# A decoder layer's second norm with its mean removed through the weights: w_down's rows centred while they are split

## The chip, the cores and the metric

The kernel runs on one core of one Trainium2 chip. The metric is the device time of one execution in microseconds (us); three runs of the kernel before gave 368.61, 368.86 and 369.11 us, and the median, 368.86 us, is the time to compare with. The engines are named as in the profile: PE is TensorE's matmul, PEld its weight load, DVE is VectorE, ACT is ScalarE, POOL is GpSimd, SP is the engine whose queue issues most transfers.

## The reference, cut to what matters

One layer over 256 positions of width 1024, all in float32. The change concerns the last two lines, the feed-forward part (FFN) and its norm:

```python
x = layer_norm(alpha * x + mix, ln1_g, ln1_b)          # first norm: its result is x1 below
u = causal_dwconv3(x @ w_up)                           # w_up 1024 x 5632
f = (silu(u[..., :2816]) * u[..., 2816:]) @ w_down     # w_down 2816 x 1024
x = layer_norm(alpha * x + f, ln2_g, ln2_b)            # second norm

def layer_norm(x, g, b):
    mu = mean(x); var = mean((x - mu) ** 2)            # over the 1024 columns
    return (x - mu) * rsqrt(var + 1e-5) * g + b
```

If each row of `w_down` has its own mean over the 1024 columns taken out, every row of `f @ w_down` has mean zero; if `alpha * x` has its mean taken out too, the sum in the second norm has mean zero, and its variance is the mean of its squares.

## The kernel before, in words

**Weights.** Float32 products are made of three matmuls in a faster type: every matrix is split in a high half `h` (a rounding copy on ACT, `split_h`) and a low half `l` (the rest, `raw - h`, on DVE, `split_l`). The weights come in 1 MB chunks of two units each, a unit being 128 x 1024 numbers: two groups of 128 columns of w_up, or two groups of 128 rows of w_down. A chunk is loaded by one transfer of SP's queue into a buffer `raw` (`issue_dma`); there are three such buffers (`RAW_BUFS = 3`), and nine for the halves (`HL_BUFS = 9`). A buffer is given to a later chunk when the instructions that read it have ended, and the loads start in the order of the list that `plan` makes.

**FFN.** The 22 groups of 128 channels are `i = 0..21`. For each, TensorE runs a gate piece (`g`, unit of chunk `ug`), a value piece (`v`, chunk `uv`) and, three groups later, a `down` (`d`, chunk `dn`) that multiplies the finished group with its 128 rows of w_down into four PSUM banks. `seq` is this list, two groups to a pair `c = 1..10`: g, v, d, g, v, d. `plan` lists the chunks of a pair as ug(c), uv(c), dn(c-1). `slot(k)` writes the work that stands beside piece k: on ACT some stages of the FFN (`fb` is the sum of the two halves of a product out of PSUM, `fc` the convolution's first tap, `fs` the silu, `f` the high half of the result), then `split_h` for the piece five ahead (six from piece 20 on), on DVE `split_l` for the piece before that, then DVE's stages. Every engine works through its own list in order. The last eight `down` (`TAIL = 8`, units of dn 7 to 10) come after all gate and value pieces.

**Second norm.** `finish(t)` handles the rows 0..127 (t = 0) and 128..255 (t = 1). For each piece of columns, DVE adds `ALPHA * x1` to the products and takes statistics (`bn_stats`); `norm_stats` joins them (`bn_aggr`) and POOL makes the power -1/2 of the variance; then come two passes of DVE, `(r - mean) * g` and `r * rstd + b`, and the transfers to `out`. For t = 1 the products of the columns 512..1023 are made last, 256 at a time (tile `e`), so that only the last 256 columns' addition and statistics, the joining and the passes follow the last matmul.

Of the kernel before, what the change touches and what calls it, by code (L numbers as in the profile page):

```python
# [8 lines left out]
F32 = mybir.dt.float32  # L9
# [6 lines left out]
P = 128  # L16
# [36 lines left out]
OFF_B, OFF_C, OFF_H, OFF_G = 3 * AW, 3 * AW + CW, 3 * AW + 2 * CW, 3 * AW + 3 * CW  # L53
TAIL = 8


def plan():

# [79 lines left out]
def layer_kernel(ctx: ExitStack, tc: tile.TileContext, x, wpack, cpack, ln1_g, ln1_b, ln2_g, ln2_b, out):  # L138
# [27 lines left out]
    raws = []  # L166
    XR_CHUNK = 20

    def issue_dma(c):
        while len(raws) <= c and len(raws) < len(chunks):  # L170
            i = len(raws)
            t = wp.tile([P, CHUNK], F32, tag="raw", name=f"raw{i}", bufs=RAW_BUFS)
            raws.append(t)
            for a, b, off in blocks[i]:
                nc.sync.dma_start(t[:, a:b], wpack[off:off + P * (b - a)].rearrange("(p n) -> p n", p=P))
            if i == XR_CHUNK:
                nc.sync.dma_start(xr, x[0].rearrange("(t p) d -> p t d", p=P))
# [5 lines left out]
    def split_start(u):  # L183
        issue_dma(units[u]["chunk"] + RAW_BUFS - 1)
        alloc(u, "h", "wh")
        alloc(u, "l", "wl")

    def split_h(u):

        issue_dma(units[u]["chunk"] + RAW_BUFS - 1)  # L190
        alloc(u, "h", "wh")
        nc.scalar.activation(units[u]["h"], raw_of(u), AF.Copy)  # L192

    def split_l(u):

        alloc(u, "l", "wl")
        nc.vector.tensor_tensor(units[u]["l"], raw_of(u), units[u]["h"].bitcast(F32), op=ALU.subtract)  # L197

    def raw_of(u):
        un = units[u]  # L200
# [524 lines left out]
        nc.vector.scalar_tensor_tensor(o, r, mv[:, 0:1], g, op0=ALU.subtract, op1=ALU.mult)  # L725
        nc.vector.scalar_tensor_tensor(o, o, mv[:, 3:4], b, op0=ALU.mult, op1=ALU.add)

    def norm_second(r, mv, ln, cs):
        nc.vector.scalar_tensor_tensor(r[:, cs], r[:, cs], mv[:, 3:4], ln[:, 1, cs], op0=ALU.mult, op1=ALU.add)

    def norm_first(r, mv, ln, cs):
        nc.vector.scalar_tensor_tensor(r[:, cs], r[:, cs], mv[:, 0:1], ln[:, 0, cs], op0=ALU.subtract, op1=ALU.mult)
# [175 lines left out]
    def take(n):  # L908
# [4 lines left out]
                pending.remove((stage, i))  # L913
        return out


    seq = []
    for c in range(1, NP // 2):
# [6 lines left out]
                seq.append(("d", d, U[("dn", d // 2)] + d % 2))  # L925
    for d in range(NP - TAIL, NP):
        seq.append(("t", d, U[("dn", d // 2)] + d % 2))
    done = {"h": cur["u"] - seq[0][2], "l": cur["u"] - seq[0][2]}
    def slot(k, stages):


        for st, i in stages:
            FFN[st][0](i)
        la = LA if k < 20 else LA + 1
        while done["h"] < min(len(seq), k + la + 2):
            split_h(seq[done["h"]][2])
            done["h"] += 1
        while done["l"] < min(len(seq), k + la + 1):
            split_l(seq[done["l"]][2])
            done["l"] += 1  # L940
        for st, i in stages:
            FFN[st][1](i)

    tail_from = next(k for k, s in enumerate(seq) if s[0] == "t")
    for k, (kind, i, u) in enumerate(seq[:tail_from]):
# [15 lines left out]
        if kind == "v":  # L961
            stages.insert(0, (0, i))
            pending.extend([(st, i) for st in (1, 2, 3)])
        slot(k, stages)


    def finish(t):
        r = x1[:, t]
        stats = tmp.tile([P, 4, 6], F32, tag="stats", name=f"rstats{t}", bufs=2)
        if t == 0:  # L970
            for k in range(TAIL):
                down(NP - TAIL + k, (t,))
                slot(tail_from + k, take(2))
            assert not pending
            for nh in range(2):
                residual(t, nh, dacc[t][nh], x1, r, stats, nh, nh * 512, nh * 512 + 512)
        else:
            for i in range(NP - TAIL, NP):
                down(i, (t,), (0,))
            nc.vector.scalar_tensor_tensor(r[:, 512:1024], x1[:, t, 512:1024], ALPHA, dacc[t][1], op0=ALU.mult, op1=ALU.add)  # L980
            for c in range(2):
                residual(t, 0, dacc[t][0], x1, r, stats, c, c * 256, c * 256 + 256)
            for c in range(2, 4):
                bank = ps_pair(f"e{c}")[:, 0]
                for i in range(NP - TAIL, NP):
                    down_part(i, bank, c)
                nc.vector.tensor_tensor(r[:, c * 256:c * 256 + 256], r[:, c * 256:c * 256 + 256], bank[:, 0:256], op=ALU.add)
                nc.vector.bn_stats(stats[:, c, :], r[:, c * 256:c * 256 + 256])
        mv = norm_stats(r, stats, 2 if t == 0 else 4)
        if t == 0:  # L990
            for c in range(2):
                cc = slice(c * 512, (c + 1) * 512)
                norm_apply(r[:, cc], r[:, cc], mv, ln2[:, 0, cc], ln2[:, 1, cc])
                nc.sync.dma_start(out[0, t * P:(t + 1) * P, cc], r[:, cc])
            return
        for c in range(2):
            norm_first(r, mv, ln2, slice(c * 512, c * 512 + 512))
        for cc, queue in ((slice(0, 640), nc.sync), (slice(640, D), nc.scalar)):
            norm_second(r, mv, ln2, cc)
            queue.dma_start(out[0, t * P:(t + 1) * P, cc], r[:, cc])  # L1000

    for t in range(2):
        finish(t)
# [42 lines left out]
```

## Time and profile before

| what | value |
|---|---|
| median of three runs | 368.86 us (368.61 to 369.11) |
| the profiled execution's own time | 369.0 us |
| its span, first to last instruction | 367.1 us |
| TensorE busy | 358.0 us, 98% of the span |
| VectorE busy | 294.9 us, 80% |
| ScalarE busy | 217.0 us, 59% |
| weight loads, 1 MB each | 55, median 4.9 us from issue to landing |

A line of the groups reads: line of the kernel, engine, operation, tile written <- tiles read, shapes, count, then busy time and mean of one in ns, then the idle time before these instructions and who ended it. A line of the timeline reads: start, duration, engine, line, operation, tiles, count, and in brackets the idle time before it with who ended it. A line of the table by stretches gives the stretch, its length, then each engine's busy time with its count of instructions (PE, PEld, DVE, ACT, POOL), the granted TensorE clock as a share of full speed, the transfers' share and GB/s. A line of the waits gives who waited for whom, the total, how often, and the longest.

### The profile page before, as it was taken

How to read it: one execution, taken by the hardware profiler on the slowest of the kernel's cores; microseconds unless marked ns; L12 is line 12 of the kernel's file. 1: busy time of each engine (PE TensorE's matmuls, PEld its weight loads, DVE VectorE, ACT ScalarE, POOL GpSimd, SP SyncE). 2: the span in 40 equal slices, each digit the busy share in tenths (PEclk: the TensorE clock that was granted, in tenths of full speed). 3: DMA queues.
4: the chain of work that ended last, by engine and by line, in shares of the span. 5: the costliest groups of instructions: out<-in, count | busy, mean ns of one | idle time of the engine just before them, and what ended most of it. 6: DMA issues, size and time to landing. Idle time of an engine off the chain costs nothing.

```text
span 367.1 us, 5335 instructions
## 1 busy us (share of the span) xinstructions
PE 358.0 (98%) x2022; PEld 312.2 (85%) x2022; DVE 294.9 (80%) x510; ACT 217.0 (59%) x372; POOL 7.0 (2%) x26
## 2 busy tenths in 40 slices
PE   8999999999999999999999999999999999999991
PEld 7888888888888899988888888888888888888891
DVE  4696887788895679869769988987869696999784
ACT  4685776747867654634266666575657566676300
POOL 2000000000000000102000000000000000000000
PEclk9999999999999999999999999999999999999998
DMA  7978565333853634596360835448182645662011
GB/s 263 356 292 318 180 225 211 114 114 129 331 214 130 221 124 137 190 357 224 124 223 12 341 121 221 153 193 309 46 334 90 254 140 204 228 237 108 0 59 57
DMA packets 11241, 69.63 MB, mean 190 GB/s; under 512 B 1232, under 2 KB 1616, under 8 KB 4176
## 3 DMA queue, kind: packets, MB, share of 16 engines
q1 hardware_dynamic: 10496, 67.00, 50.0%
q0 software_dynamic: 576, 2.10, 1.8%
q8 instruction: 16, 0.26, 0.3%
q10 hardware_dynamic: 144, 0.20, 0.1%
q14 instruction: 9, 0.07, 0.1%
HBM read 68.24 MB, written 1.05 MB: 189 GB/s over the span
## 4 chain that ended last, share of the span: by engine, by line
PE 97%; DVE 1%; DMA 1%; DVEq 0%; SPq 0%; issue 0%
PE pb L333 20%; PE pb L340 10%; PE g L333 8%; PE d L305 5%; PE d L306 5%; PE d L307 5%; PE g L340 4%; PE q L555 3%; PE k L555 3%; PE v L555 3%; PE b L333 2%; PE y L326 2%; PE y L325 2%; PE y L324 2%; PE c L333 2%; PE o L307 2%
## 5 line engine op out<-in xcount | busy, mean ns | idle before, releaser
L197 DVE TENSOR_TENSOR wl<-raw,wh 128x1024 fp32r<-128x1024 f32 x90 | 109.8, 1221 | 23.3 <-ACT wh L192 22.7
L192 ACT ACTIVATE wh<-raw 128x1024 fp32r<-128x1024 f32 x90 | 94.5, 1055 | 22.7 <-DMA raw<-in_wpack 22.6
L333 PE MATMUL pb<-x1T,wh 128*128 128x512 f32 x320 | 76.2, 390 | 0.0
L333 PEld LDWEIGHTS pb<-x1T,wh 128*128 128x128 f32 x320 | 59.7, 188 | 12.1
L220 DVE TENSOR_TENSOR wl<-raw,wh 128x1024 fp32r<-128x1024 f32 (+1 forms) x38 | 38.0, 1037 | 7.4 <-ACT wh L219 7.1
L340 PEld LDWEIGHTS pb<-x1T,wl 128*128 128x128 f32 x320 | 41.0, 191 | 1.6
L340 PE MATMUL pb<-x1T,wl 128*128 128x256 f32 x320 | 41.5, 283 | 0.0
L219 ACT ACTIVATE wh<-raw 128x1024 fp32r<-128x1024 f32 (+1 forms) x38 | 32.9, 904 | 14.3 <-DMA raw<-in_wpack 8.5
L333 PE MATMUL g<-xT,wh 128*128 128x512 f32 x128 | 31.4, 393 | 0.0
L305 PE MATMUL d<-wh,f 128*128 128x512 f32 x80 | 31.3, 391 | 0.0
L306 PE MATMUL d<-wl,f 128*128 128x512 f32 x80 | 31.3, 391 | 0.0
L307 PE MATMUL d<-wh,f 128*128 128x512 f32 x80 | 31.1, 389 | 0.0
L333 PEld LDWEIGHTS g<-xT,wh 128*128 128x128 f32 x128 | 23.3, 188 | 4.5
L807 ACT ACTIVATE fb<-pb 128x512 f32<-128x512 f32 x20 | 11.9, 595 | 23.8 <-PE pb L340 23.8
L825 DVE SCALAR_TENSOR_TENSOR fc<-fb,consts,fc 128x254 f32<-128x254 f32 x40 | 19.3, 484 | 1.4
L823 DVE SCALAR_TENSOR_TENSOR fc<-fb,consts,fc 128x255 f32<-128x255 f32 x40 | 19.1, 478 | 0.0
L817 ACT ACTIVATE fc<-fb,consts 128x256 f32<-128x256 f32 x40 | 17.9, 496 | 0.4 <-DVE fb L811 0.4
L307 PEld LDWEIGHTS d<-wh,f 128*128 128x128 f32 x80 | 15.0, 188 | 3.2
L305 PEld LDWEIGHTS d<-wh,f 128*128 128x128 f32 x80 | 15.1, 189 | 2.7
L306 PEld LDWEIGHTS d<-wl,f 128*128 128x128 f32 x80 | 15.1, 189 | 2.6
L340 PEld LDWEIGHTS g<-xT,wl 128*128 128x128 f32 x128 | 16.4, 191 | 0.6
L340 PE MATMUL g<-xT,wl 128*128 128x256 f32 x128 | 16.6, 283 | 0.0
(183 smaller groups left out, 606.1 us busy)
## 6 DMA issues: line engine op xcount, KB each, us to landing
raw<-in_wpack SPq DMA_DIRECT2D x55, 1024.0 KB, 4.9
raw<-in_wpack SPq DMA_DIRECT2D x6, 896.0 KB, 5.5
xr<-in_x SPq DMA_DIRECT2D x1, 1024.0 KB, 7.6
ln<-in_ln_g POOLq DMA_DIRECT2D x2, 512.0 KB, 5.6
ln<-in_ln_b POOLq DMA_DIRECT2D x2, 512.0 KB, 6.2
raw<-in_wpack SPq DMA_DIRECT2D x3, 256.0 KB, 3.4
raw<-in_wpack SPq DMA_DIRECT2D x1, 512.0 KB, 5.8
out<-x SPq DMA_DIRECT2D x2, 256.0 KB, 2.1
```

The source lines that it names most:

```text
L192: nc.scalar.activation(units[u]["h"], raw_of(u), AF.Copy)
L197: nc.vector.tensor_tensor(units[u]["l"], raw_of(u), units[u]["h"].bitcast(F32), op=ALU.subtract)
L219: nc.scalar.activation(h, src, AF.Copy)
L220: (eng or nc.vector).tensor_tensor(l, src, h.bitcast(F32), op=ALU.subtract)
L305: nc.tensor.matmul(o, ah, bh, start=start, stop=False)
L306: nc.tensor.matmul(o, ah, bl, start=False, stop=False)
L307: nc.tensor.matmul(o, al, bh, start=False, stop=stop)
L333: nc.tensor.matmul(bank, un["h"][:, k, :], b[:, k].rearrange("p a s -> p (a s)"), start=k == 0, stop=False)
L340: nc.tensor.matmul(bank[:, 0:S], un["l"][:, k, :], b[:, k, 0], start=False, stop=k == nk - 1)
L555: nc.tensor.matmul(banks[m][t], (xl if p == 2 else xh)[:, k, t * P:(t + 1) * P], wl if p == 1 else wh, start=k == 0 and p == 0, stop=k == ...
L823: nc.vector.scalar_tensor_tensor(c[:, 1:S], pb[:, a * S:a * S + S - 1], w_ffn(1, j), c[:, 1:S], op0=ALU.mult, op1=ALU.add)
L825: nc.vector.scalar_tensor_tensor(c[:, 2:S], pb[:, a * S:a * S + S - 2], w_ffn(0, j), c[:, 2:S], op0=ALU.mult, op1=ALU.add)
```

## The change

1. `split_h` of a w_down unit first makes a pass of ACT over the raw unit with `scale = -1/D` and an accumulator (`row_means`), which leaves minus the mean of each row in a small tile `wm`; the copy then becomes `Identity` with that tile as its bias. `split_l` of such a unit becomes `(raw + m) - h`, one instruction of DVE with three operands.
2. For the last eight units (dn 7 to 10) the sums are not made at their split. `plan` lists a second load of the same chunk ahead of the pairs c = 2, 4, 6, 8 (`SUMS`), and `early_means` makes the two passes over it, each ahead of a `split_h` in the list of ACT. The passes write over the raw data they read. These units keep only the bias at their own split.
3. `centred(t)`, after the pieces 14 and 17, scales x1 by `ALPHA` in place on ACT with an accumulator over the row, and a small second instruction makes minus the mean (`XM`).
4. In `finish` the addition is `(bank + XM) + x1`, the statistics are sums of squares (`squares`, with EPS as the start value, each piece starting from the piece before), the factors `g` are multiplied in by piece (`times_factors`), POOL's power works on the last sum, and one pass, `r * rstd + b`, remains with the transfers (`store`). `norm_second` and `norm_first` are gone.

```diff
+SUMS = {2: 7, 4: 8, 6: 9, 8: 10}
...
     for c in range(1, NP // 2):
+        if c in SUMS:
+            mark(("sum", SUMS[c]))
+            rows("w_dn", 2 * SUMS[c])
         mark(("ug", c))
...
+    CENTRED = {U[("dn", d)] + e for d in range(NP // 2) for e in range(2)}
...
+    def row_means(u, raw, o, tag):
+        units[u]["m"] = tmp.tile([P, 1], F32, tag=tag, name=f"wm{u}", bufs=8)
+        nc.scalar.activation(o, raw, AF.Copy, scale=-1.0 / D, accum_out=units[u]["m"])
+
+    def early_means(d, e):
+        v = U[("sum", d)] + e
+        issue_dma(units[v]["chunk"] + RAW_BUFS - 1)
+        row_means(U[("dn", d)] + e, raw_of(v), raw_of(v), "wt")
...
     def split_h(u):
...
-        nc.scalar.activation(units[u]["h"], raw_of(u), AF.Copy)
+        h, raw = units[u]["h"], raw_of(u)
+        if u in CENTRED:
+            if "m" not in units[u]:
+                row_means(u, raw, h, "wm")
+            nc.scalar.activation(h, raw, AF.Identity, bias=units[u]["m"])
+        else:
+            nc.scalar.activation(h, raw, AF.Copy)
     def split_l(u):
...
+        if u in CENTRED:
+            nc.vector.scalar_tensor_tensor(units[u]["l"], raw_of(u), units[u]["m"], units[u]["h"].bitcast(F32),
+                                           op0=ALU.add, op1=ALU.subtract)
...
+    def centred(t):
+        m = tmp.tile([P, 2], F32, tag="xm", name=f"xm{t}", bufs=2)
+        nc.scalar.activation(x1[:, t], x1[:, t], AF.Copy, scale=ALPHA, accum_out=m[:, 0:1])
+        nc.scalar.activation(m[:, 1:2], m[:, 0:1], AF.Copy, scale=-1.0 / D)
+        XM[t] = m[:, 1:2]
...
+    for c, d in SUMS.items():
+        k = [u for _, _, u in seq].index(U[("ug", c)])
+        early[k - 1], early[k] = (d, 0), (d, 1)
...
         while done["h"] < min(len(seq), k + la + 2):
+            if done["h"] in early:
+                early_means(*early[done["h"]])
             split_h(seq[done["h"]][2])
...
+        if k in (14, 17):
+            centred((k - 14) // 3)
...
+    def add_residual(t, cc, bank):
+        nc.vector.scalar_tensor_tensor(x1[:, t, cc], bank, XM[t], x1[:, t, cc], op0=ALU.add, op1=ALU.add)
+
+    def squares(t, cc, var, c):
+        r = x1[:, t, cc]
+        n = cc.stop - cc.start
+        nc.vector.tensor_tensor_reduce(out=scratch([P, n], f"sq{t}{c}"), in0=r, in1=r, scale=1.0 / D,
+                                       scalar=var[:, c - 1:c] if c else EPS, op0=ALU.mult, op1=ALU.add,
+                                       accum_out=var[:, c:c + 1])
+
+    def times_factors(t, cc):
+        nc.vector.scalar_tensor_tensor(x1[:, t, cc], x1[:, t, cc], 1.0, ln2[:, 0, cc], op0=ALU.mult, op1=ALU.mult)
+
+    def store(t, cc, rstd, queue):
+        r = x1[:, t, cc]
+        nc.vector.scalar_tensor_tensor(r, r, rstd, ln2[:, 1, cc], op0=ALU.mult, op1=ALU.add)
+        queue.dma_start(out[0, t * P:(t + 1) * P, cc], r)
...
-                nc.vector.bn_stats(stats[:, c, :], r[:, c * 256:c * 256 + 256])
-        mv = norm_stats(r, stats, 2 if t == 0 else 4)
+                squares(t, cc, var, c - 1)
+                if c == 2:
+                    times_factors(t, cc)
+        last = 1 if t == 0 else 2
+        nc.gpsimd.tensor_tensor(var[:, 3:4], var[:, last:last + 1], neghalf, op=ALU.pow)
...
+            times_factors(t, slice(768, D))
+            store(t, slice(0, 640), rstd, nc.sync)
+            store(t, slice(640, D), rstd, nc.scalar)
```

In the order in which the instructions stand on each engine, TensorE's list is unchanged. In a pair with a sum chunk ACT's list reads: first pass over the sum chunk, pass and copy of a w_down unit, second pass over the sum chunk, copy of the gate unit, copy of the value unit, pass and copy of the next w_down unit. The load of that pair's value chunk takes the buffer of the sum chunk and waits on ACT's second pass.

More of the change, by code (lines that the diff above doesn't have):

```diff
@@ L914, in take @@
         return out
+    XM = {}
+    def centred(t):
[3 more added lines that the diff above has]
+        XM[t] = m[:, 1:2]
     seq = []
@@ L974, in finish @@
             assert not pending
-            for nh in range(2):
-                residual(t, nh, dacc[t][nh], x1, r, stats, nh, nh * 512, nh * 512 + 512)
+            for c, cc in enumerate(halves):
+                add_residual(t, cc, dacc[t][c])
+                squares(t, cc, var, c)
+                times_factors(t, cc)
         else:
```

37 lines of the change are left out of this document (16 added, 21 removed).

## The prediction

> **What bounds the kernel now.** I read the page first, its first lines and the chain that ended last, then the table by stretches, the waits, and the timelines of ScalarE (ACT), VectorE (DVE) and the load queue (SP) inside the FFN stage.
>
> ```profile
> PE 358.0 (98%) x2022; PEld 312.2 (85%) x2022; DVE 294.9 (80%) x510; ACT 217.0 (59%) x372; POOL 7.0 (2%) x26
> PE 97%; DVE 1%; DMA 1%; DVEq 0%; SPq 0%; issue 0%
> ```
> ```profile
> 240.00:280.00 40.00, 40.00 (x210) 34.43 (x209) 33.03 (x50) 25.74 (x41) 0.00 (x0) 1.00 0.51 189
> ...
> 360.00:367.10 7.10, 0.00 (x0) 0.00 (x0) 3.42 (x6) 0.00 (x0) 0.55 (x1) 0.83 0.20 74
> ```
>
> TensorE is the chain (97%), without a hole from the first weights on; behind it stands a tail of some 7.7 us in which VectorE finishes the second norm and the output leaves. So a change pays in two ways only: it shortens the tail, or it makes TensorE wait, and each microsecond of waiting is added whole. In the FFN stage ACT is busy 25.74 of 40 us and looks as if it had room. The waits say what the rest is:
>
> ```profile
> ACT fb L807 <- PE pb L340: 23.8, 16, 2.8
> ACT wh L192 <- DMA raw<-in_wpack: 22.6, 16, 2.9
> ```
>
> ACT also waits for weight loads, because only three raw buffers exist and a load starts when its buffer's last low half is made. Parts of the FFN stage (ACT; two load issues on SP; two low halves on DVE; TensorE's pace; the `down` in which TensorE uses those low halves):
>
> ```profile
> 269.37 1.06 ACT L192 ACTIVATE wh<-raw 128x1024 fp32r<-128x1024 f32 x1 [1.38 <-DMA raw<-in_wpack]
> 273.23 1.06 ACT L192 ACTIVATE wh<-raw 128x1024 fp32r<-128x1024 f32 x1 [2.49 <-DMA raw<-in_wpack]
> 275.65 1.06 ACT L192 ACTIVATE wh<-raw 128x1024 fp32r<-128x1024 f32 x1 [0.58 <-DMA raw<-in_wpack]
> 276.62 0.89 ACT L817 ACTIVATE fc<-fb,consts 128x256 f32<-128x256 f32 x2
> 277.42 1.05 ACT L192 ACTIVATE wh<-raw 128x1024 fp32r<-128x1024 f32 x1
> ...
> 326.19 0.60 ACT L807 ACTIVATE fb<-pb 128x512 f32<-128x512 f32 x1 [1.66 <-PE pb L340]
> 326.69 0.41 ACT L830 ACTIVATE fs<-fc 128x256 f32<-128x256 f32 x1
> 327.00 1.05 ACT L192 ACTIVATE wh<-raw 128x1024 fp32r<-128x1024 f32 x1
> ```
> ```profile
> 264.57 0.33 SPq L175 DMA_DIRECT2D raw<-in_wpack  x1
> 266.04 0.33 SPq L175 DMA_DIRECT2D raw<-in_wpack  x1
> ```
> ```profile
> 199.42 1.22 DVE L197 TENSOR_TENSOR wl<-raw,wh 128x1024 fp32r<-128x1024 f32 x1
> ...
> 270.46 1.23 DVE L197 TENSOR_TENSOR wl<-raw,wh 128x1024 fp32r<-128x1024 f32 x1 [0.19 <-ACT wh L192]
> ```
> ```profile
> 268.05 3.63 PE pb L333 x16
> 271.68 1.91 PE pb L340 x16
> ...
> 284.62 3.63 PE pb L333 x16
> ```
> ```profile
> 207.13 0.40 PE L305 MATMUL d<-wh,f 128*128 128x512 f32 x1
> ...
> 281.71 0.40 PE L305 MATMUL d<-wh,f 128*128 128x512 f32 x1
> ```
>
> Three things are read here. First, the steps of ACT from start to start: a split 0.97 (275.65 to 276.62), fb 0.50, fs 0.31 (f, of the same shape, is taken alike), the two fc 0.80. Second, a load's time from issue to use: 4.80 when nothing went just before it (264.57 to 269.37), 7.19 for the second of a burst (266.04 to 273.23). Third, the cushion: a pair of FFN pieces takes TensorE 16.57 us (268.05 to 284.62), that is twice 3.63 + 1.91 = 5.54 for gate and value columns (the wide passes of either 1.82, the narrow ones of both 1.91) and twice 2.75 for a `down`; the low half that ends at 271.69 is multiplied at 281.71, so 10.0 us lie between, but only 6.5 in the second pair (200.64 to 207.13). That cushion is all that protects TensorE.
>
> **The change part by part.** (1) Every row of w_down gets a pass over 128x1024 on ACT that sums it (22 passes), the split gets a bias from memory, the low half becomes a three-operand instruction on DVE. The nearest rows for summing and for a pointer operand:
>
> ```profile
> 68.02 0.50 ACT L424 ACTIVATE sm<-sm,st 128x256 f32<-128x256 f32 x1
> 68.42 0.19 ACT L424 ACTIVATION_READ_ACCUMULATOR sm<-sm,st 128x1 f32 x1
> 68.52 0.50 ACT L424 ACTIVATE sm<-sm,st 128x256 f32<-128x256 f32 x1
> ```
> ```profile
> L655 ACT ACTIVATE gates<-gs,consts 128x256 f32<-128x256 f32 x16 | 7.9, 504 | 0.4 <-DVE gs L652 0.2
> L830 ACT ACTIVATE fs<-fc 128x256 f32<-128x256 f32 x22 | 9.0, 410 | 4.5 <-DVE fc L825 4.5
> L725 DVE SCALAR_TENSOR_TENSOR x<-xr,mv,ln 128x512 f32<-128x512 f32 x4 | 3.0, 756 | 0.1
> L742 DVE SCALAR_TENSOR_TENSOR xr<-xr,o 128x512 f32<-128x512 f32 x4 | 2.7, 680 | 2.7 <-PE o L307 2.7
> ```
>
> The accumulator read starts 0.40 after its instruction and the next instruction 0.10 later, so a summing pass takes 0.97 + 0.10 = 1.07 of ACT's time, or 0.97 + 0.19 = 1.16 until its sum can be used; a pointer costs 0.09 (504 less 410). Sum and split that waits for it: 1.16 + 1.15 = 2.3 in place of 1.06. On DVE a pointer costs 0.08 (756 less 680); 22 of them are 1.8 us under an engine that is 83% busy in this stage, and it hides except in the chains below. The lower bound for a summing pass is that it takes no longer than the 0.97 (accumulator read hidden); the upper is a full serial 1.06 + 0.19 = 1.25. I keep 1.07 and 1.16, the nearest rows.
>
> (2) Four more loads of 1 MB (before pairs 2, 4, 6, 8), each in the same three raw buffers, and two summing passes over each (m0, m1). The queue is in order and the DMA share is 0.51, so bytes are no limit. Buffers are. In such a pair ACT's order is m0, sum and split of a w_down half, m1, split of the gate columns, split of the value columns. Four chunks now pass three buffers: the value columns' load gets the buffer of the sum chunk, so it can start only when m1 is done, and ACT needs it two operations later. And m0, with everything behind it on ACT, waits for the sum chunk's load. Before, neither wait was there. Behind the value load SP holds the next w_down load, whose buffer comes free later still, so that wait costs nothing more.
>
> Pair 6, counted from the moment the low half of the preceding `down` unit is done (0), with a cushion of 0.7 us then: the sum load is issued when the next low half is done, 1.3 to 1.8 (one low half of 1.23 and at most half a microsecond of other DVE work), and lands after 5.2 (4.80 alone, a little more since another load went 1.5 before), at 6.75. m0 1.07, sum and split 2.3, low half 1.27: 11.4. TensorE wants that unit at 2.75 + 5.54 + 0.7 = 9.0 (one `down` slot, one gate-value piece): **it stands 2.4**. fs 0.31 and m1 to its sum 1.16: 11.6. The value load: 16.4; split 17.45. TensorE, back at 11.4, has done `down` 2.75 and the gate's wide passes 1.82 and is at 15.95: **1.5**. Then 3.73 of value passes, to 21.2, while ACT does fc 0.80, sum and split 2.3, DVE the low half 1.27, to 21.8: **0.6**. Together 4.5, and the cushion is then zero.
>
> A pair without a sum chunk: load 4.80, sum and split 2.3, low half 1.3 is 8.4 against 8.3, so 0.1 stands; then 3.86 of ACT steps (fs, split, fb, f, split, two fc) and another 2.3 and 1.3 end at 14.5, 2.1 before TensorE: a cushion of 2.1 at its end. Pair 8 starts with that: 1.0 + 1.5 + 0.6 = 3.1. Pair 2 starts with 6.5, of which its own loop of 21.8 against 16.57 takes 5.2: no stall, 1.3 left. Pair 3 regains 1.1, not 2.1: in the order of this early part the two fc and the four DVE instructions that wait for them stand ahead of the low half that frees its value columns' buffer, about 1 us. It ends with 2.4. Pair 4 pays 0.7 at m0, and since fb, f and two fc (1.59 in place of 0.31) stand ahead of its m1, 2.75 at the value columns, 0.6 after: 4.05. (3) The two passes over x1 (`centred`, 1.07 + 0.19 + about 0.2 = 1.5 each) lie in pairs 4 and 5 and leave the 0.7 used above instead of 2.1. Sum: 4.05 + 0.1 + 4.5 + 0.1 + 3.1 = **11.9 us of TensorE standing still**.
>
> (4) The tail. Of the two norms at the end only what follows the last matmul counts:
>
> ```profile
> 359.42 0.42 DVE L987 TENSOR_TENSOR x<-x,e 128x256 f32<-128x256 f32 x1 [2.00 <-PE e L307]
> 359.88 0.43 DVE L988 BATCH_NORM_STATS2 rstats<-x 128x6 f32<-128x256 f32 x1
> 360.34 0.26 DVE L720 BATCH_NORM_AGGREGATE mv<-rstats 128x2 f32<-128x24 f32 x1
> 360.64 1.44 DVE L732 SCALAR_TENSOR_TENSOR x<-x,mv,ln 128x512 f32<-128x512 f32 x2
> 362.18 1.41 DVE L729 SCALAR_TENSOR_TENSOR x<-x,mv,ln 128x640 f32<-128x640 f32 x2
> ```
> ```profile
> 350.81 0.55 POOL L721 TENSOR_TENSOR mv<-mv,neghalf 128x1 f32<-128x1 f32 x1 [173.11 <-DVE mv L720]
> ...
> 360.68 0.55 POOL L721 TENSOR_TENSOR mv<-mv,neghalf 128x1 f32<-128x1 f32 x1 [9.32 <-DVE mv L720]
> ```
> ```profile
> 351.64 0.75 DVE L726 SCALAR_TENSOR_TENSOR x<-x,mv,ln 128x512 f32<-128x512 f32 x1
> ```
> ```profile
> L413 DVE CUSTOM_DVE_ANT_0 sm<-s,mask 128x256 f32<-128x256 f32 x8 | 3.0, 418 | 0.0
> L413 DVE DVE_READ_ACCUMULATOR2_ANT st<- 128x1 f32 x16 | 1.3, 82 | 0.0
> ```
>
> New: after the add, squares 0.42 + 0.08, ready at 360.40; POOL's power starts 0.08 later, takes 0.55, and DVE follows 0.28 after it (351.36 to 351.64): 361.3. The product with the factors of the last 256 columns (about 0.42) fits beside the power. The last instructions start at 361.3, not 362.18: **0.9 less**; no engine but DVE, POOL and the two output queues is in that stretch. Work taken from the aggregate and the two passes over 512 columns at 360.64 moves ahead of 359.42, where DVE waited 2.00 us.
>
> The sum goes by the profiled execution's 369.0 us, its span of 367.1 and 1.9 around it (median of the runs 368.86, 0.04% off): 369.0 + 11.9 - 0.9 = **380.0 us**.
>
> **The clock.** The granted clock is 1.00 in the stretch of dense matmuls above and 0.83 in the last 7.1 us, which hold none. The Trainium skill (TensorE: Matmul & The Clock Gate, Part 1) says why a hole could cost more than its length: after about 3.4 us of idleness the array falls to half rate and needs about as long a busy time to come back. By it each forecast hole (2.75 at most) is too short, and the sum stays; the next paragraph's second rival is the case where it does not.
>
> **The rivals.** *The cushion is enough.* Decides if ACT can run on past the sum chunk, so that the lag per pair stays below what is regained; then only the tail moves: 369.0 - 0.9 = 368.1. For it: 10.0 us of cushion late in the stage, ACT at 64% (25.74 of 40). Against it: two serial loads of 4.8 in one pair of 16.57. Chance 0.08. *Burst loads and a slower clock.* The sum loads come at 7.19 like the second of a burst (2.0 more in three pairs), holes grow over 3.4, and in each of these pairs one `down` slot of 2.75 runs at half rate: 3 x (2.0 + 2.75) = 14 more, 394 with both, 386 to 394 with part of it. Chance 0.17. *Half the stall.* The summing passes cost nothing beyond a split and DVE's low halves never queue: about 0.3 less at each of twelve steps and the start's 10.0 of cushion instead of 6.5 gives 380 - 4 - 3 = 373. Chance 0.15. The forecast, 376 to 386: 0.60.
>
> **How the numbers follow.** The time is the forecast's. The range, 373 to 389, leaves out the first rival and the upper half of the second. A measurement here can tell about 0.2% (0.7 us) from no change; 368.1 is 0.2% below, so the first rival's 0.08 splits into 0.05 faster and 0.03 same; all else, 0.92, is slower.
>
> **What would show it.** TensorE's row in the stretches from 218 us on below full, with holes at a `down`, a value piece and a `down` of pairs 4, 6 and 8, none in pair 2; ACT waiting for loads ahead of the new summing passes and ahead of the value split, far over 22.6 us in all; SP waiting for ACT, four times; the tail's last pass 1.9 us after the last add's start instead of 2.76. It is wrong if TensorE's row stays full, or if the holes stand at other operations, such as the gate pieces waiting for a PSUM bank that a late fb holds.

## The result, and the profile after

The changed kernel takes 393.31 us (median; 391.90 to 393.92) beside 368.91 us (368.61 to 369.11) of the kernel before on the same chip: 1.066 times as long, 95% interval 1.0637 to 1.0683. The forecast was 380.0 us in 373 to 389: slower as said, by twice as much as said. The profiled execution took 393.52 us, its span 391.7 us.

The page of the kernel after, its busy times, the granted clock over 40 slices, and the chain that ended last:

```profile
PE 369.8 (94%) x2022; PEld 317.3 (81%) x2022; DVE 295.2 (75%) x510; ACT 244.5 (62%) x422; POOL 7.7 (2%) x26
...
PEclk9999999999999999999989999999699969899999
...
PE 44%; DMA 20%; DVE 16%; ACT 11%; issue 6%; SPq 0%; POOL 0%; POOLq 0%; DVEq 0%; ACTq 0%
```

TensorE was 97% of the chain and is 44% now; loads are 20% of it, VectorE and ScalarE 27%. The span grew by 24.6 us. TensorE's busy time grew by 11.8 of them (369.8 less 358.0) for the same 2022 matmuls, so 12.8 are standing still and 11.8 are longer matmuls. By the mean granted clock, 0.972 over 391.7 us and 0.997 over 367.1 before, some 10 of these 11.8 are a lower clock (an estimate: 11.0 less 1.1).

The waits of the kernel after, those that were absent or smaller before:

```profile
DVE wl L221 <- ACT wh L213: 31.6, 10, 7.2
ACT wh L215 <- DMA raw<-in_wpack: 19.8, 10, 3.2
...
ACT raw L198 <- DMA raw<-in_wpack: 16.6, 4, 6.1
```

ACT waits for loads 16.6 us ahead of the four m0 passes (`raw`, L198), 19.8 ahead of plain splits, and 3.1 more ahead of the passes that a w_down unit has at its own split: 39.5 in all, where it was 22.6.

Where TensorE falls behind is read from the start of the same piece in both TensorE timelines:

| piece | before | after | behind by |
|---|---|---|---|
| d0 | 198.85 | 202.13 | 3.28 |
| gate piece after d0 | 201.59 | 206.82 | 5.23 |
| gate piece ahead of d8 | 259.60 | 264.85 | 5.25 |
| d8 | 265.14 | 274.11 | 8.97 |
| gate piece after d8 | 267.89 | 280.29 | 12.40 |
| gate piece ahead of d12 | 292.75 | 306.16 | 13.41 |
| d12 | 298.29 | 314.70 | 16.41 |
| gate piece after d12 | 301.04 | 320.88 | 19.84 |
| gate piece after d13 | 309.32 | 329.56 | 20.24 |
| addition after the last matmul | 359.42 | 385.17 | 25.75 |

The loss comes in four steps: at d0 (second load of pair 2) 5.2, around d8 (pair 6) 7.2 and 1.0 more until d12, from d12 (pair 8) to the gate piece after d13 6.8, behind it 5.5 (the last five groups' gate and value pieces, and the tail). Pair 4 loses nothing.

One step closely, pair 6, in the timelines after: three load issues, ACT, and TensorE; and between them the table by stretches (columns as in the table before).

```profile
261.58 0.33 SPq L182 DMA_DIRECT2D raw<-in_wpack  x1
263.05 0.33 SPq L182 DMA_DIRECT2D raw<-in_wpack  x1
265.12 0.33 SPq L182 DMA_DIRECT2D raw<-in_wpack  x1
```
```profile
263.50:271.00 7.50, 7.05 (x39) 5.99 (x37) 3.35 (x7) 1.22 (x3) 0.00 (x0) 1.00 0.99 394
```
```profile
270.69 1.06 ACT L198 ACTIVATE raw<-raw 128x1024 f32<-128x1024 f32 x1 [6.12 <-DMA raw<-in_wpack]
...
271.75 1.04 ACT L198 ACTIVATE wh<-raw 128x1024 fp32r<-128x1024 f32 x1
...
272.91 1.15 ACT L213 ACTIVATE wh<-raw,wm 128x1024 fp32r<-128x1024 f32 x1
...
274.27 1.04 ACT L198 ACTIVATE raw<-raw 128x1024 f32<-128x1024 f32 x1
...
280.29 1.06 ACT L215 ACTIVATE wh<-raw 128x1024 fp32r<-128x1024 f32 x1 [3.15 <-DMA raw<-in_wpack]
```
```profile
274.11 0.79 PE L332 MATMUL d<-wh,f 128*128 128x512 f32 x1 [3.56 <-ACT wh L213]
275.43 0.79 PE L333 MATMUL d<-wl,f 128*128 128x512 f32 x1 [0.53 <-DVE wl L221]
```

The sum chunk is issued at 263.05, between two other loads, and read at 270.69: 7.64 us, in which the transfers are busy 0.99 of the time. Three megabytes go at once, and the first pass waits for the second of them. ACT waits 6.12 us for it, with d8's split behind in its list, and TensorE stands 3.56 us until that split is made. Then m1 ends at about 275.4, and only now, with nothing else under way, the value columns' load goes; it comes some 4.9 us later. ACT's prices are as forecast: 1.06 a summing pass (270.69 to 271.75; 1.07 said), 1.16 to its sum's use (271.75 to 272.91; 1.16 said).

The granted clock after the holes, in the same table of the kernel after:

```profile
202.10:205.30 3.20, 3.09 (x7) 2.00 (x8) 3.13 (x7) 3.17 (x6) 0.00 (x0) 0.51 0.00 0
274.10:280.30 6.20, 5.66 (x13) 4.09 (x14) 3.77 (x5) 3.05 (x7) 0.00 (x0) 0.50 0.45 170
314.70:320.90 6.20, 5.59 (x13) 4.07 (x14) 3.76 (x5) 3.21 (x7) 0.00 (x0) 0.51 0.48 169
338.70:342.20 3.50, 3.50 (x10) 2.69 (x9) 3.43 (x8) 2.51 (x4) 0.00 (x0) 0.51 0.63 201
```

Half rate: the slot of d8 takes 6.2 us (274.11 to 280.29, 0.53 of it a hole) in place of 2.75.

The tail, from the timeline after:

```profile
385.17 0.42 DVE L1048 TENSOR_TENSOR x<-x,e 128x256 f32<-128x256 f32 x1 [1.47 <-PE e L334]
...
386.20 0.79 POOL L1053 TENSOR_TENSOR var<-var,neghalf 128x1 f32<-128x1 f32 x1 [8.11 <-DVE var L1012]
387.02 1.42 DVE L1021 SCALAR_TENSOR_TENSOR x<-x,var,ln 128x640 f32<-128x640 f32 x2 [0.44 <-POOL var L1053]
```

From the addition to the start of the last passes 1.85 us, where it was 2.76 (359.42 to 362.18).

### The profile page after: what moved, and what is told of

The parts are those of the page before. It is cut to its first block, busy times and chain, and to the rows that moved or that the text cites. A ratio compares the mean times of both kernels' runs of the same rounds, so it can differ in the third digit from the quotient of the medians.

```text
span 391.7 us, 5384 instructions
## 1 busy us (share of the span) xinstructions
PE 369.8 (94%) x2022; PEld 317.3 (81%) x2022; DVE 295.2 (75%) x510; ACT 244.5 (62%) x422; POOL 7.7 (2%) x26
## 4 chain that ended last, share of the span: by engine, by line
PE 44%; DMA 20%; DVE 16%; ACT 11%; issue 6%; SPq 0%; POOL 0%; POOLq 0%; DVEq 0%; ACTq 0%
DMA raw<-in_wpack 20%; PE g L360 8%; DVE wl L224 5%; PE g L367 4%; DVE wl L221 3%; ACT wh L213 3%; ACT wh L198 2%; PE q L582 2%; PE k L582 2%; PE v L582 2%; ACT raw L198 2%; DVE fc L844 2%; DVE fc L846 2%; PE b L360 2%; PE y L353 2%
## 5 line engine op out<-in xcount | busy, mean ns | idle before, releaser
L224 DVE TENSOR_TENSOR wl<-raw,wh 128x1024 fp32r<-128x1024 f32 x68 | 83.0, 1221 | 20.0 <-ACT wh L215 19.8
L215 ACT ACTIVATE wh<-raw 128x1024 fp32r<-128x1024 f32 x68 | 71.4, 1055 | 19.8 <-DMA raw<-in_wpack 19.8
L360 PE MATMUL pb<-x1T,wh 128*128 128x512 f32 x320 | 78.7, 399 | 2.8 <-DVE fb L832 2.8
L360 PEld LDWEIGHTS pb<-x1T,wh 128*128 128x128 f32 x320 | 61.4, 194 | 16.4 <-DVE fb L832 3.4
L221 DVE SCALAR_TENSOR_TENSOR wl<-raw,wm,wh 128x1024 fp32r<-128x1024 f32 x22 | 28.2, 1282 | 31.6 <-ACT wh L213 31.6
L332 PE MATMUL d<-wh,f 128*128 128x512 f32 x80 | 34.3, 428 | 9.2 <-ACT wh L213 6.4
L333 PE MATMUL d<-wl,f 128*128 128x512 f32 x80 | 34.2, 428 | 1.9 <-DVE wl L221 1.9
L334 PE MATMUL d<-wh,f 128*128 128x512 f32 x80 | 33.8, 423 | 0.1
L332 PEld LDWEIGHTS d<-wh,f 128*128 128x128 f32 x80 | 16.4, 205 | 12.8 <-ACT wh L213 6.8
L213 ACT ACTIVATE wh<-raw,wm 128x1024 fp32r<-128x1024 f32 x22 | 25.2, 1147 | 0.5
L333 PEld LDWEIGHTS d<-wl,f 128*128 128x128 f32 x80 | 16.6, 207 | 6.6 <-DVE wl L221 3.7
L334 PEld LDWEIGHTS d<-wh,f 128*128 128x128 f32 x80 | 16.4, 205 | 4.4 <-DVE f L862 0.9
L198 ACT ACTIVATE raw<-raw 128x1024 f32<-128x1024 f32 x8 | 8.4, 1052 | 16.6 <-DMA raw<-in_wpack 16.6
```

The costliest lines, as they stand in the source:

```text
L213: nc.scalar.activation(h, raw, AF.Identity, bias=units[u]["m"])
L215: nc.scalar.activation(h, raw, AF.Copy)
L221: nc.vector.scalar_tensor_tensor(units[u]["l"], raw_of(u), units[u]["m"], units[u]["h"].bitcast(F32), op0=ALU.add, op1=ALU.subtract)
L332: nc.tensor.matmul(o, ah, bh, start=start, stop=False)
L333: nc.tensor.matmul(o, ah, bl, start=False, stop=False)
L334: nc.tensor.matmul(o, al, bh, start=False, stop=stop)
```

## The experiments

The theory after the result: a fourth chunk in a ring of three buffers makes loads wait for one another, and TensorE follows the ring. Its rivals: ACT's extra passes; the clock, to which some 10 us of the 24.6 go; the transfers' own bytes. The kernel before gave medians of 368.3 to 368.9 us in these comparisons.

### What each part costs by itself

`no_second_load`: every row is summed at its own split.

```diff
-SUMS = {2: 7, 4: 8, 6: 9, 8: 10}
+SUMS = {}
```

> The four second loads and their eight summing passes are gone; the last eight units are summed at their own split, all else of the change stays. Theory (a sum chunk in a ring of three buffers makes ACT wait for two loads in a row): the waits of ACT for loads fall back to the 22.6 us in all of the kernel before, TensorE has no hole from 187 us to the end, the granted clock stays 1.00 there, and only the tail's 0.9 us is left: 368.0 us (367.5 to 369.5). Rival (the summing passes themselves fill ACT; 22 of 1.07 us plus the waits for their sums): most of the 24 us stays, 385 us or more.

Measured 372.30 us, 1.0109 (1.0060 to 1.0158). The first tail `down` starts at 336.61 (before 337.13), so nothing is lost until there. The loss is in the last eight, four holes of TensorE:

```profile
345.00 0.51 PE L333 MATMUL d<-wl,f 128*128 128x512 f32 x1 [0.81 <-DVE wl L221]
347.00 0.50 PE L332 MATMUL d<-wh,f 128*128 128x512 f32 x1 [0.57 <-ACT wh L213]
348.35 0.50 PE L333 MATMUL d<-wl,f 128*128 128x512 f32 x1 [0.85 <-DVE wl L221]
350.85 0.50 PE L333 MATMUL d<-wl,f 128*128 128x512 f32 x1 [0.52 <-DVE wl L221]
```

A tail `down` takes TensorE half of a 2.75 slot, a sum with its split takes ACT 2.2 us. So without second loads the 14 other summing passes hide whole, and 368.0 was wrong by the eight in the tail.

`tail_alone`: the new end of the second norm and the two passes over x1, with the weights as before.

```diff
-SUMS = {2: 7, 4: 8, 6: 9, 8: 10}
+SUMS = {}
...
-    CENTRED = {U[("dn", d)] + e for d in range(NP // 2) for e in range(2)}
+    CENTRED = set()
```

> No row of w_down is summed or centred here and no second load is issued; the split of w_down and the ring are those of the kernel before, and only the new end (factors by piece, squares in place of the aggregate) and the two passes over x1 are left. It leaves the mean of the feed-forward part in the second norm. If the tail is worth the 0.9 us that the prediction gave it and the two passes over x1 cost nothing by themselves: 368.0 us, ratio 0.9975. If the two passes over x1 alone already made TensorE wait: 369 or more, with a hole between 230 and 270 us.

Measured 367.76 us, 0.9972 (0.9955 to 0.9990): faster by some 1.0 us, as the tail's term says. It is the one kernel faster than the one before, but it leaves the mean of the feed-forward part in the second norm, so it is no version to use.

`loads_alone`: the kernel before, with the four second loads in the ring and a read of one column in place of a sum.

```diff
+    def early_read(d, e):
+        v = U[("sum", d)] + e
+        issue_dma(units[v]["chunk"] + RAW_BUFS - 1)
+        t = cst.tile([P, 1], F32, name=f"wt{v}")
+        nc.scalar.activation(t, raws[units[v]["chunk"]][:, units[v]["off"]:units[v]["off"] + 1], AF.Copy)
```

> The kernel before, with nothing of the change but the four second loads in the ring, each unit read by one column on ACT where the summing passes stand. No centring, old tail. Theory: the two waits for loads per sum pair make most of the delay by themselves; a sum pair's loop is then 7.2 + 0.2 + 1.1 + 0.3 + 0.2 + 4.8 + 1.0 + 0.8 + 1.1 + 0.3 + 1.1 + 1.3 = 19.4 us against 16.57, a pair without about 11, so the cushion is regained in full each time: 370 to 375 us, with holes only at the first down, 0 and 8, 12. Rival (the ring alone costs as much as the whole change): 385 us or more. If it is 369, the ring hurts only together with the summing passes.

Measured 376.57 us, 1.0230 (1.0207 to 1.0252), above the 370 to 375 expected, and the holes stand elsewhere: at gate pieces that wait for DVE's fb addition (the longest 2.47 us, at 318.82) and at a `down` in the tail, none over 0.3 us at the first down, 8 or 12.

`loads_small_reads` is the changed kernel with the same one-column reads; the last eight units are summed at their own split.

```diff
-        row_means(U[("dn", d)] + e, raw_of(v), raw_of(v), "wt")
+        t = tmp.tile([P, 1], F32, tag="wt", name=f"wt{v}", bufs=8)
+        nc.scalar.activation(t, raws[units[v]["chunk"]][:, units[v]["off"]:units[v]["off"] + 1], AF.Copy)
```

> The four second loads stay and so do the two waits on them, but ACT reads one column of each unit in place of a pass over it (the sums of the last eight units are made at their own split). Theory (the waits for the loads, not the work, make the delay): each pair with a sum chunk is shorter by the two passes, 2 x 0.9 us, about 4 x 1.8 = 7 us less in all at most: 386 us (383 to 391). Rival (ACT's work in those pairs): close to 369 us.

Measured 390.20 us, 1.0565 (1.0510 to 1.0619). That is 3 us less than the changed kernel, but the median hides two shifts, because these last eight units now pay in the tail as in no_second_load. The first tail `down` here, then in the changed kernel:

```profile
354.58 0.40 PE L333 MATMUL d<-wh,f 128*128 128x512 f32 x1
```
```profile
361.52 0.40 PE L332 MATMUL d<-wh,f 128*128 128x512 f32 x1
```

Ahead of the tail the eight early passes cost 6.9 us, as expected, and 17.5 of the 24.4 us by which the changed kernel is late there (337.13 before) stay without them; from there to the last addition this kernel takes 26.6 us (354.58 to 381.14), the changed one 23.7 (361.52 to 385.17). So the waits for the loads are the larger part, and the passes, which stand in the same chain, are not free. The parts do not add up: summing alone costs 3.6 us (372.30 less 368.71, the new tail's gain included), the loads alone 8.2 (376.57 less 368.33), both together 24.4. The likely reason, which no run separates, is that each uses up the same cushion: the serial loads take it in half the pairs, and the slower split (2.2 us for 1.06) takes what the other pairs would give back.

### The clock

`keep_warm`: ten matmuls of zeros ahead of the pieces that stood, so that the array isn't idle there.

```diff
+    def busy(bank, start, n=10):
+        for _ in range(n):
+            nc.tensor.matmul(bank.rearrange("p (a s) -> p a s", a=4), zeros, zeros[:, None, :].to_broadcast([P, 4, P]),
+                             start=start, stop=start)
+
+    WARM = {("d", 0), ("d", 8), ("v", 12), ("d", 12), ("v", 16), ("g", 18)}
```

> Ten matmuls of zeros (10 x 0.23 us) stand on TensorE ahead of each of six pieces at which it stood still or would stand still at full clock (down 0, 8 and 12, value 12 and 16, gate 18), so that the holes are no longer idle; they add zero to an open sum or go into a bank that is started anew. If the half clock behind the holes (11.7 us of longer matmuls) is time of its own, the kernel takes 382 us (380 to 386). If the chain of loads, ACT and DVE sets the pace and slow matmuls only fill what would be further holes, it stays within 2 us of the 393.3.

Measured 394.61 us, 1.0703 (1.0662 to 1.0744): no gain. TensorE and ACT at the same place, in this kernel:

```profile
272.06 2.33 PE L982 MATMUL d<-zeros 128*128 128x512 bf16 x10
...
275.84 0.49 PE L333 MATMUL d<-wl,f 128*128 128x512 f32 x1 [0.82 <-DVE wl L221]
...
278.67 2.11 PE L360 MATMUL pb<-x1T,wh 128*128 128x512 f32 x8
...
286.56 0.40 PE L332 MATMUL d<-wh,f 128*128 128x512 f32 x1
```
```profile
272.00:280.00 8.00, 7.02 (x30) 4.19 (x30) 3.78 (x5) 5.51 (x11) 0.00 (x0) 1.00 0.41 141
```
```profile
280.64 1.06 ACT L215 ACTIVATE wh<-raw 128x1024 fp32r<-128x1024 f32 x1 [3.10 <-DMA raw<-in_wpack]
```

At full clock this `down` ends 2.8 us after its low half's hole (275.84 to 278.67), against 4.9 in the changed kernel (275.43 to 280.29). But the value columns' load comes at 280.64 all the same, and d9 starts at 286.56, there at 286.03. Most of what full rate saves is waited for at the next load. Here ten zeros stand in that wait and outlast it by 0.9 us (the split ends at 281.70, the value passes start at 282.61); at v16 and g18 the zeros end some 2.0 and 0.8 us after what the piece waits for. So this run could hide a few microseconds of saving, and it gives back only part of the clock (mean 0.988: some 3.6 us more lost than before, where the changed kernel lost 9.9).

The four runs of the changed kernel, which have no zeros, say the same. The one with a mean clock of 0.986 took 393.92 us, the one with 0.968 took 391.90, although by these figures 7 us less of the first went to the lower clock (5.5 us of its span of 392.1, 12.5 of 390.1). So the slow matmuls are in the main not a cost beside the waits: they fill time in which TensorE would have stood. A rest of a few microseconds is not excluded.

### Order and place of the passes

`passes_together`: both passes behind the split, not around it, so that the buffer comes free at once.

```diff
-            if done["h"] in early:
-                early_means(*early[done["h"]])
             split_h(seq[done["h"]][2])
+            if done["h"] in early and early[done["h"]][1] == 0:
+                for e in range(2):
+                    early_means(early[done["h"]][0], e)
```

> The changed kernel with both passes over a sum chunk placed right behind the split of the w_down unit, in place of one before it and one a piece later. The sum load no longer holds up that unit, and the value columns' load starts about one piece (1.5 to 2.5 us) earlier. Theory: each sum pair's loop is shorter by the time that the w_down unit's sum and split (2.3) now fill while the sum load is on its way, and by what stood before the second pass: 3 x 2.5 to 3 x 4 us, 381 to 386 us, holes smaller at down 8 and 12. Rival (only the number of passes and loads counts): 393 us.

Measured 383.19 us, 1.0401 (1.0373 to 1.0430). Order alone gives back 10 us of the 24: the split that TensorE waits for is no longer behind the wait for the sum chunk, and the sum chunk's buffer comes free sooner. The largest hole left is at a gate piece:

```profile
327.43 1.06 PE L360 MATMUL pb<-x1T,wh 128*128 128x512 f32 x2 [3.72 <-DVE fb L832]
```

### A buffer beside the ring

`own_buffer`: the second loads go to the place of `xr`, free after the first norm, and the ring keeps its own chunks.

```diff
+    def sum_load(d):
+        (a, b, off), = blocks[units[U[("dn", d)]]["chunk"]]
+        OWN[d] = big.tile([P, 2, D], F32, tag="x", name=f"own{d}")
+        nc.sync.dma_start(OWN[d], wpack[off:off + P * (b - a)].rearrange("(p t n) -> p t n", p=P, t=2))
```

> The second loads go into a buffer of their own (the place that the first norm's input leaves free), so the ring of three raw buffers runs as in the kernel before; all summing passes, their order on ACT and the bytes loaded are those of the changed kernel. Theory (the ring): the two serial waits are gone, TensorE has at most a hole under 1 us at the first down, 368 to 369.5 us. Rival (ACT's work, or the bytes): above 380 us.

`own_spaced`: the same with one pass a pair.

```diff
-        early[k - 1], early[k] = (d, 0), (d, 1)
+        early[k] = (d, 0)
+        early[[u for _, _, u in seq].index(U[("ug", c + 1)])] = (d, 1)
```

> As own_buffer, but one early summing pass in each of the pairs 2 to 9 in place of two in every second pair. ACT's work per pair is even. Theory: the same as own_buffer or up to 0.5 us less, 368.0 us, that is the tail's 0.9 us below the kernel before. Rival as there.

`own_late`: passes one pair later, loads of half the size, each issued behind the ring's load.

```diff
-SUMS = {2: 7, 4: 8, 6: 9, 8: 10}
+SUMS = {3: 7, 5: 8, 7: 9, 9: 10}
...
             split_h(seq[done["h"]][2])
+            if done["h"] in early and early[done["h"]][0] < NP // 2 - 1:
+                d, e = early[done["h"]]
+                sum_load(d + 1, e)
```

> Second loads in a buffer of their own as in own_spaced, but one pair later (passes in pairs 3 to 10, none in pair 2), in loads of half the size, each issued behind the ring's load and not ahead of it. If what own_spaced still lost (372.97) came from the pass in pair 2 and from 1 MB loads that stood ahead of ring loads (holes of 0.67, 0.29 and 0.64 us, VectorE late until 350 us and a hole of 1.43 us there): 368.0 to 369.5 us, no hole over 0.3 us before the tail. If the passes on ScalarE themselves take the cushion: 372 to 373 us again, with the holes at other places.

Measured: own_buffer 375.15 us, 1.0203 (1.0155 to 1.0251); own_spaced 372.97, 1.0131 (1.0109 to 1.0153); own_late 378.86, 1.0262 (1.0234 to 1.0291). The first two recover 18 and 20 us, but miss the 368 to 369.5 expected of them. In own_buffer TensorE stands at d0:

```profile
202.92 0.68 PE L339 MATMUL d<-wh,f 128*128 128x512 f32 x1 [4.68 <-ACT f L865]
```

ACT waits 4.49 us for the first second load (until 193.85), and what f needs, and then f, which d0 needs, stand behind that in its list. own_late has no hole there, and fell elsewhere; its ACT, DVE and TensorE ahead of the largest hole:

```profile
318.80 1.06 ACT L219 ACTIVATE wh<-raw 128x1024 fp32r<-128x1024 f32 x1 [2.52 <-DMA raw<-in_wpack]
```
```profile
319.88 1.22 DVE L228 TENSOR_TENSOR wl<-raw,wh 128x1024 fp32r<-128x1024 f32 x1 [2.32 <-ACT wh L219]
321.03 0.68 DVE L836 TENSOR_TENSOR fb<-pb,fb 128x512 f32<-128x512 f32 x1
```
```profile
321.77 0.80 PE L364 MATMUL pb<-x1T,wh 128*128 128x512 f32 x1 [3.11 <-DVE fb L836]
```

Three loads of the ring (issued at 309.47, 310.94 and 313.01) and one of half a megabyte (309.85) are under way together; the table by stretches has the transfers busy 0.98 of the next 6 us:

```profile
312.00:318.00 6.00, 6.00 (x33) 5.18 (x33) 4.29 (x7) 2.86 (x6) 0.00 (x0) 1.00 0.98 384
```

The ring's load is late by that, ACT and DVE wait with it, and DVE's addition that empties a PSUM pair stands behind the low half: TensorE has no bank for the next gate piece. In this trace half a megabyte among the ring's loads goes with that; but own_late changed the place of the loads, their size and the pairs of the passes at once, and no run separates the three. Both cases of its expectation (368 to 369.5 and 372 to 373 us) were missed.

### One buffer more

`four_raw`: four raw buffers for the whole kernel, paid with one of the nine buffers of halves.

```diff
-    RAW_BUFS, HL_BUFS = 3, 9
+    RAW_BUFS, HL_BUFS = 4, 8
```

> A fourth raw buffer, paid for with one of the nine buffers of the halves; instructions and loads are those of the changed kernel. Theory: the value columns' load no longer waits for the second summing pass and the sum load starts a chunk earlier, so the holes of TensorE go: 368 to 372 us. Rival (ACT's work or the transfers' share is too much): 385 us or more. If eight buffers for the halves were too few, TensorE would wait for halves evenly in all pairs, those without a sum chunk too.

Measured 372.83 us, 1.0105 (1.0086 to 1.0125). This is just above the 372 expected. In the FFN stage only 0.29 us stands, at d0. The rest is lost ahead of it, in the first norm: one of TensorE's holes, and ACT's wait ahead of it, for which the profile shows no releaser:

```profile
172.21 0.63 PE L807 MATMUL x1t<-ident,x 128*128 128x128 f32 x4 [0.83 <-DVE x L753]
```
```profile
164.66 1.06 ACT L246 ACTIVATE wh<-raw 128x1024 fp32r<-128x1024 f32 x1 [8.82 <-issue]
```

The kernel before makes this split at 157.13. Here its low half keeps DVE from the first norm until 166.90 (162.74 before). four_ring, which keeps nine buffers for the halves, has neither wait, so that eight are too few is the likely cause.

`four_ring`: the fourth buffer is xr's place, from the first second load on; nothing else differs from the changed kernel.

```diff
+    X0 = plan_units[U[("sum", 7)]][0]
+
+    def ring_to(c):
+        return c + RAW_BUFS if c + RAW_BUFS >= X0 else c + RAW_BUFS - 1
...
-            t = wp.tile([P, CHUNK], F32, tag="raw", name=f"raw{i}", bufs=RAW_BUFS)
+            if i >= X0 and (i - X0) % 4 == 0:
+                t = big.tile([P, CHUNK], F32, tag="x", name=f"raw{i}")
+            else:
+                t = wp.tile([P, CHUNK], F32, tag="raw", name=f"raw{i}", bufs=RAW_BUFS)
...
-        issue_dma(units[u]["chunk"] + RAW_BUFS - 1)
+        issue_dma(ring_to(units[u]["chunk"]))
```

> The changed kernel with a fourth buffer in the ring from the first second load on: the place of xr, which is free after the first norm. Everything before that, and the nine buffers of high and low halves, stay. If the whole loss is the ring's fourth chunk in three buffers, TensorE stands nowhere before the tail and only the tail's 0.9 us is left: 368.0 to 368.8 us. If a cost of the second loads is left that a buffer doesn't cure (their bytes in front of the ring's, the passes on ScalarE, or VectorE's longer low halves at the end): 370 to 373 us, with holes at d0 and at the last down units as in the two kernels with a buffer of their own.

Measured 368.91 us, 1.0007 (0.9993 to 1.0021): the loss is gone but for some 0.8 us ahead of the tail, with every pass, every byte and the order of ACT as in the changed kernel. Its page:

```profile
PE 358.8 (98%) x2022; PEld 311.7 (85%) x2022; DVE 294.7 (80%) x510; ACT 244.4 (67%) x422; POOL 7.7 (2%) x26
...
PE 92%; issue 3%; DVE 3%; ACT 1%; POOL 0%; POOLq 0%; DVEq 0%; ACTq 0%
```

and ACT at pair 6's first pass, with its waits for loads:

```profile
257.87 1.06 ACT L205 ACTIVATE raw<-raw 128x1024 f32<-128x1024 f32 x1 [1.82 <-DMA raw<-in_wpack]
```
```profile
ACT raw L205 <- DMA raw<-in_wpack: 4.9, 3, 1.8
ACT wh L222 <- DMA raw<-in_wpack: 4.7, 3, 1.9
```

With 1.1 us more at the w_down units' own passes ACT waits 10.7 us for loads here, in the changed kernel 39.5, in the kernel before 22.6. The first tail `down` starts at 337.93, 0.8 behind the kernel before; the new tail takes 0.9 back. It does not beat the kernel before.

`four_ring_late`: the same, with the second loads before pairs 3, 5, 7 and 9.

```diff
-SUMS = {2: 7, 4: 8, 6: 9, 8: 10}
+SUMS = {3: 7, 5: 8, 7: 9, 9: 10}
```

> The same with the second loads before pairs 3, 5, 7 and 9 in place of 2, 4, 6 and 8; the fourth buffer joins one pair later. If a hole at d0 is all that four buffers leave in the pairs: faster than the other by that hole, 368.0 us. If the tail's down units come short of low halves because the last passes lie nearer to them: 1 to 2 us slower than the other, with the hole at a down on a low half behind 340 us.

Measured 370.61 us, 1.0048 (1.0029 to 1.0067), so the second of its two cases: no hole at d0, but one of 0.63 us at a `down` in the tail (347.65), where the last sums are nearer.

## Why the prediction was right and wrong

**The bound and the ring held.** TensorE was the chain, the cushion was the raw buffers', and four chunks passing three buffers made ACT and then TensorE wait: four_ring, which changes only that, takes the loss away but for 0.8 us. ACT waits ahead of m0 and the value split as said, SP waits for ACT four times, and TensorE has holes at a `down` of pairs 6 and 8. The holes forecast at the value piece and at the second `down` of these pairs (1.5 and 0.6 us) did not come: the half-rate slot ahead of them took up that time. In keep_warm, at full rate, the value split of pair 6 ends 1.1 us after the gate's passes (280.63, 281.70).

**The price of ACT's and DVE's new work was right.** A summing pass 1.06 (1.07 said), a sum and its split 2.2 (2.3 said), the low half with a pointer 1.28 (1.27 said). Without second loads they cost nothing until the tail; no_second_load shows what they cost there, 4.7 us between its first tail `down` and the last addition, if the last eight are not made early. In the chain of the second loads the early passes cost 6.9 us (loads_small_reads).

**The tail was right**: 1.85 us to the last passes in place of 2.76, and 367.76 us when it stands alone (368.1 said for that case). POOL's power took 0.79 and not 0.55, but DVE followed 0.82 us after its start, where the sum had 0.83.

**The sum of 11.9 us of standing was wrong; 25.75 were lost ahead of the tail's last addition, standing and slow matmuls together.** By its steps:

- Pair 2, "no stall": 5.2 us. The forecast followed the weights and left out f. At d0 TensorE waits for the high half of f, which stands on ACT behind the value columns' split and so behind their load. The ACT and TensorE timelines after:

```profile
200.72 1.06 ACT L215 ACTIVATE wh<-raw 128x1024 fp32r<-128x1024 f32 x1 [3.15 <-DMA raw<-in_wpack]
201.68 0.40 ACT L858 ACTIVATE f<-ff 128x256 fp32r<-128x256 f32 x1
```
```profile
202.13 0.78 PE L332 MATMUL d<-wh,f 128*128 128x512 f32 x1 [2.75 <-ACT f L858]
```

- Pair 4, 4.05 said: nothing. Its sum load took 5.26 us (224.01 to 229.27), as forecast, but the 5.2 us lost at d0 are cushion won for the loads, and pair 4 lives on them. keep_warm bears this out: there TensorE leaves d0 2.2 us earlier (204.66 for 206.82), and stands in pair 4 at the value piece, where the forecast had put 2.75:

```profile
241.79 3.05 PE L360 MATMUL pb<-x1T,wh 128*128 128x512 f32 x8 [2.00 <-ACT wh L215]
```

- Pairs 6 and 8, 4.5 and 3.1 said: 7.2 and 6.4. The term that was mis-sized is the sum chunk's load, 5.2 us taken, 7.64 measured in pair 6 (263.05 to 270.69) and 7.18 in pair 8 (304.10 to 311.28). The prediction reasoned that a load 1.5 us ahead adds little to 4.80, but it had the row of a burst, 7.19, and this load, like that one, goes between two others. They are issued 1.5 us before and 2.1 after it in pair 6, and 2.2 before and 3.0 after it in pair 4, where 5.2 was right. That is the first half of the rival "burst loads and a slower clock", whose 386 to 394 us hold the measured time. The prediction also said of the loads that "bytes are no limit", from a DMA share of 0.51 over 40 us; in the burst the share is 0.99.
- Behind the gate piece after d13, nothing said: 5.5 us. A low half waiting for its load held DVE's fb addition and with it a PSUM pair, which the prediction named as a sign of being wrong; TensorE and DVE after:

```profile
335.64 1.23 DVE L224 TENSOR_TENSOR wl<-raw,wh 128x1024 fp32r<-128x1024 f32 x1 [1.31 <-ACT wh L215]
336.79 0.68 DVE L832 TENSOR_TENSOR fb<-pb,fb 128x512 f32<-128x512 f32 x1
```
```profile
337.52 5.55 PE L360 MATMUL pb<-x1T,wh 128*128 128x512 f32 x16 [2.27 <-DVE fb L832]
```

- The clock, "each forecast hole is too short": it fell to 0.50 after holes of 2.75, 3.56, 2.85 and 2.27 us. The half of the rival that adds 2.75 us for each slow slot is not borne out either: by keep_warm and the four runs of the changed kernel, the slow matmuls cost little beside the loads that TensorE waits for. The Trainium skill (TensorE: Matmul & The Clock Gate, Part 1) gives about 3.4 us of idleness as the window, and says that the window runs freely; three of the four holes are shorter than it, so the trace does not bear out its use as a lower bound.

What stays open: how the 10 us that passes_together gave back divide between the split's place and the earlier release, how much of the 5.5 us at the end is clock, and which of own_late's three changes made it slower than own_spaced.

## What to carry to other kernels

When a change puts a chunk more into a ring of load buffers, lay out each load's issue, its landing and the pass that frees its buffer, and count the ring's turn against the consumer's; shares of ACT and of the transfers (64% and 0.51 here) say nothing on it. Price a load in a burst by a row of a burst, follow everything that stands behind the waiting instruction on its engine (f and fb here, not the weights alone), and try one buffer more before moving work: here it was worth 24 us, and a buffer beside the ring 18 to 20. The Trainium skill (Perfetto Trace Analysis, Optimization Strategy) reads a gap that repeats on the engine that should be full as a possible sign of too few buffers; the holes at d8 and d12, the same operation two pairs later, and four_ring agree.

## What the runs showed of the hardware

In the changed kernel holes of TensorE of 2.27 to 3.56 us were followed by 3.2 to 6.2 us at a granted clock of 0.50 to 0.51; after the one of 2.27 us the clock stayed at 1.00 for 1.2 us more (337.52 to 338.70) and fell then. In keep_warm a hole of 2.00 us was followed by 0.50 as well (242.80 to 245.80). But not every hole was: after 2.32 us in own_late and 2.47 us in loads_alone the clock stayed at 1.00, and after 3.11 us in own_late it was 0.50. The table by stretches of own_late, then of loads_alone:

```profile
270.40:273.40 3.00, 3.00 (x13) 2.50 (x14) 2.66 (x5) 2.97 (x6) 0.00 (x0) 1.00 0.00 0
321.80:324.30 2.50, 2.50 (x6) 2.02 (x7) 2.46 (x5) 1.92 (x4) 0.00 (x0) 0.50 0.02 7
```
```profile
318.80:322.00 3.20, 3.18 (x14) 2.65 (x15) 3.13 (x7) 2.62 (x5) 0.00 (x0) 1.00 0.27 38
```

So the length of a hole between 2.0 and 2.9 us does not by itself tell whether the clock falls. A load of a megabyte took 7.64 us between two others close to it, with transfers at 394 GB/s and a share of 0.99, and 4.9 us from issue to use with no other under way (275.43 to 280.29).
